# Huber loss of two 8192 x 8192 arrays: row tiles in bf16 over three engines, replaced by flat tiles in f32 on one transfer queue

## The chip, the cores and the metric

The kernel runs on one core of a Trainium2 chip. The metric is the device time of one execution in microseconds. A core has the engines DVE (vector), ACT (scalar functions), POOL (general purpose) and PE (matrix, not used here), and SP, which only issues transfers. Each engine works through its own list of instructions in order. Transfers between HBM and the on-chip memory (128 partitions) run on 16 transfer engines, fed from the queues of SP, ACT and POOL.

## The reference

```python
def reference(pred, target):
    delta = 1.0
    diff = pred - target
    abs_diff = np.abs(diff)
    return np.where(abs_diff <= delta, 0.5 * diff**2, delta * (abs_diff - 0.5 * delta))
```

Both inputs and the output are 8192 x 8192 f32, 268.44 MB each. So 536.87 MB are read and 268.44 MB written, and there are three or four elementwise steps per element. Both kernels compute 0.5 * min(|d|, 1)^2 + max(|d| - 1, 0), with d = pred - target.

## The kernel before

The arrays are taken in 64 row tiles of 128 rows x 8192 columns. A row tile is loaded in two halves of 4096 columns for each input (`emit_loads`, L46; 2.1 MB each, in f32). The first input and the first half of the second are issued by SP (L54, L56), the second half of the second by ACT. Each input has a pool of three such half buffers. POOL subtracts the halves into one bf16 tile `dfull` (L103), so everything behind it is in half precision. `dfull` has two buffers, the result tile `sfull` three.

For a row tile ACT takes the absolute value of `dfull` in place (L108) and DVE writes min(|d|, 1) to `sfull` (L109). One round later, in `do_tail` (L65), ACT squares `sfull` with the factor sqrt(0.5) (L68), ACT writes max(|d| - 1, 0) to `dfull` (L69) and DVE adds the two (L70). The store of `sfull` goes out from POOL's queue (L63), which casts it from bf16 to f32 on the way, a round later still.

Thus ACT's list in a round is L68 and L69 of one tile, then L108 of the next. L68 of that next tile waits for DVE's L109. POOL's subtraction needs a free `dfull`, that is, the end of L70 two tiles earlier; and SP's next loads need half buffers that POOL has read.

The last two row tiles (L117 to L226) are written out by hand in pieces of 2048 or 1024 columns, spread over ACT and DVE, so that the last stores are small.

Of the kernel before, what the change touches and what calls it, by code (L numbers as in the profile page):

```python
# [6 lines left out]


@with_exitstack
def kernel(  # L10
# [6 lines left out]
    nc = tc.nc  # L17
    P = 128
    fp32 = mybir.dt.float32
    bf16 = mybir.dt.bfloat16  # L20
    Alu = mybir.AluOpType
    Act = mybir.ActivationFunctionType

    n_rows, n_cols = pred.shape
    COLS = 4096
    n_ct = n_cols // COLS
    SQRT_HALF = 0.70710678118654752

    pred_t = pred.rearrange("(n p) m -> n p m", p=P)
    targ_t = target.rearrange("(n p) m -> n p m", p=P)  # L30
    out_t = out.rearrange("(n p) m -> n p m", p=P)
    n_rt = pred_t.shape[0]

    neg1 = nc.alloc_sbuf_tensor("huber_neg1_bf16", [P, 1], bf16)
    nc.gpsimd.memset(neg1.ap(), -1.0)

    pool_a = ctx.enter_context(tc.tile_pool(name="sbuf_a", bufs=3))
    pool_b = ctx.enter_context(tc.tile_pool(name="sbuf_b", bufs=3))
    pool_d = ctx.enter_context(tc.tile_pool(name="sbuf_d", bufs=2))
    pool_s = ctx.enter_context(tc.tile_pool(name="sbuf_s", bufs=3))  # L40

    loads = {}
    pending_tail = []
    pending_store = []

    def emit_loads(i):  # L46
        if i >= n_rt:
            return
        tl = []
        for j in range(n_ct):  # L50
            c0 = j * COLS
            a = pool_a.tile([P, COLS], fp32)
            b = pool_b.tile([P, COLS], fp32)
            nc.sync.dma_start(out=a, in_=pred_t[i, :, c0 : c0 + COLS])  # L54
            beng = nc.sync if j == 0 else nc.scalar
            beng.dma_start(out=b, in_=targ_t[i, :, c0 : c0 + COLS])  # L56
            tl.append((a, b))
        loads[i] = tl

    def flush(limit):  # L60
        while len(pending_store) > limit:
            r, pi = pending_store.pop(0)
            nc.gpsimd.dma_start(out=out_t[pi, :, :], in_=r)  # L63

    def do_tail(limit):  # L65
        while len(pending_tail) > limit:
            s, d, pi = pending_tail.pop(0)
            nc.scalar.activation(out=s, in_=s, func=Act.Square, scale=SQRT_HALF)  # L68
            nc.scalar.activation(out=d, in_=d, func=Act.Relu, bias=neg1.ap())  # L69
            nc.vector.tensor_tensor(out=s, in0=s, in1=d, op=Alu.add)  # L70
            pending_store.append((s, pi))

    def act_path(d, s):
        nc.scalar.activation(out=d, in_=d, func=Act.Abs)
        nc.vector.tensor_scalar(
            out=s, in0=d, scalar1=1.0, scalar2=None, op0=Alu.min
        )
        nc.scalar.activation(out=s, in_=s, func=Act.Square, scale=SQRT_HALF)
        nc.scalar.activation(out=d, in_=d, func=Act.Relu, bias=neg1.ap())
        nc.vector.tensor_tensor(out=s, in0=s, in1=d, op=Alu.add)  # L80

    def dve_path(d, s):
        nc.vector.tensor_scalar(
            out=s, in0=d, scalar1=-1.0, scalar2=1.0, op0=Alu.max, op1=Alu.min
        )
        nc.vector.scalar_tensor_tensor(
            out=d, in0=s, scalar=-0.5, in1=d, op0=Alu.mult, op1=Alu.add
        )
        nc.vector.tensor_tensor(out=s, in0=s, in1=d, op=Alu.mult)

    emit_loads(0)
    for i in range(n_rt - 2):
        dfull = pool_d.tile([P, n_cols], bf16)
        sfull = pool_s.tile([P, n_cols], bf16)

        emit_loads(i + 1)

        do_tail(0)

        for j in range(n_ct):  # L100
            c0 = j * COLS
            a, b = loads[i][j]
            nc.gpsimd.tensor_tensor(  # L103
                out=dfull[:, c0 : c0 + COLS], in0=a, in1=b, op=Alu.subtract
            )
        del loads[i]

        nc.scalar.activation(out=dfull, in_=dfull, func=Act.Abs)  # L108
        nc.vector.tensor_scalar(  # L109
            out=sfull, in0=dfull, scalar1=1.0, scalar2=None, op0=Alu.min,  # L110
        )

        flush(1)

        pending_tail.append((sfull, dfull, i))

    i62 = n_rt - 2  # L117
    i63 = n_rt - 1
    H = n_cols // 2

    d62 = pool_d.tile([P, n_cols], bf16, tag="dfull")
    s62 = pool_s.tile([P, n_cols], bf16, tag="sfull")

    emit_loads(i63)
    do_tail(0)

    for j in range(n_ct):
        c0 = j * COLS
        a, b = loads[i62][j]
        nc.gpsimd.tensor_tensor(  # L130
            out=d62[:, c0 : c0 + COLS], in0=a, in1=b, op=Alu.subtract
        )
    del loads[i62]

    flush(1)

    Q = 2048
    dq = [d62[:, k * Q : (k + 1) * Q] for k in range(4)]
    sq = [s62[:, k * Q : (k + 1) * Q] for k in range(4)]
    nc.scalar.activation(out=dq[0], in_=dq[0], func=Act.Abs)  # L140
    nc.vector.tensor_scalar(out=sq[0], in0=dq[0], scalar1=1.0, scalar2=None, op0=Alu.min)  # L141
    nc.vector.tensor_scalar(  # L142
        out=sq[1], in0=dq[1], scalar1=-1.0, scalar2=1.0, op0=Alu.max, op1=Alu.min
    )
    nc.scalar.activation(out=sq[0], in_=sq[0], func=Act.Square, scale=SQRT_HALF)  # L145
    nc.scalar.activation(out=dq[0], in_=dq[0], func=Act.Relu, bias=neg1.ap())
    nc.vector.scalar_tensor_tensor(  # L147
        out=dq[1], in0=sq[1], scalar=-0.5, in1=dq[1], op0=Alu.mult, op1=Alu.add
    )
    nc.vector.tensor_tensor(out=sq[0], in0=sq[0], in1=dq[0], op=Alu.add)  # L150
    nc.scalar.activation(out=dq[2], in_=dq[2], func=Act.Abs)
    nc.vector.tensor_tensor(out=sq[1], in0=sq[1], in1=dq[1], op=Alu.mult)  # L152
    nc.vector.tensor_scalar(out=sq[2], in0=dq[2], scalar1=1.0, scalar2=None, op0=Alu.min)  # L153
    nc.vector.tensor_scalar(
        out=sq[3], in0=dq[3], scalar1=-1.0, scalar2=1.0, op0=Alu.max, op1=Alu.min
    )
    nc.scalar.activation(out=sq[2], in_=sq[2], func=Act.Square, scale=SQRT_HALF)  # L157
    nc.scalar.activation(out=dq[2], in_=dq[2], func=Act.Relu, bias=neg1.ap())  # L158
    nc.vector.scalar_tensor_tensor(  # L159
        out=dq[3], in0=sq[3], scalar=-0.5, in1=dq[3], op0=Alu.mult, op1=Alu.add  # L160
    )
    nc.vector.tensor_tensor(out=sq[2], in0=sq[2], in1=dq[2], op=Alu.add)  # L162
    nc.vector.tensor_tensor(out=sq[3], in0=sq[3], in1=dq[3], op=Alu.mult)

    d63 = pool_d.tile([P, n_cols], bf16, tag="dfull")
    s63 = pool_s.tile([P, n_cols], bf16, tag="sfull")

    bounds = [0, 2048, 4096, 6144, 7168, 8192]
    chunks = [(bounds[k], bounds[k + 1]) for k in range(len(bounds) - 1)]

    flush(0)
    for k, (lo, hi) in enumerate(chunks):
        a, b = loads[i63][lo // COLS]
        o0, o1 = lo % COLS, (hi - 1) % COLS + 1
        nc.gpsimd.tensor_tensor(  # L175
            out=d63[:, lo:hi], in0=a[:, o0:o1], in1=b[:, o0:o1], op=Alu.subtract
        )
        if 1 <= k <= 4:
            nc.gpsimd.dma_start(  # L179
                out=out_t[i62, :, (k - 1) * Q : k * Q], in_=sq[k - 1]  # L180
            )
    del loads[i63]

    d0, s0 = d63[:, 0:2048], s63[:, 0:2048]
    d1, s1 = d63[:, 2048:4096], s63[:, 2048:4096]
    d2, s2 = d63[:, 4096:6144], s63[:, 4096:6144]
    d3, s3 = d63[:, 6144:7168], s63[:, 6144:7168]
    d4, s4 = d63[:, 7168:8192], s63[:, 7168:8192]

    def st(lo, hi, s):  # L190
        nc.gpsimd.dma_start(out=out_t[i63, :, lo:hi], in_=s)  # L191

    nc.scalar.activation(out=d0, in_=d0, func=Act.Abs)
    nc.vector.tensor_scalar(out=s0, in0=d0, scalar1=1.0, scalar2=None, op0=Alu.min)  # L194
    nc.scalar.activation(out=s0, in_=s0, func=Act.Square, scale=SQRT_HALF)  # L195
    nc.scalar.activation(out=d0, in_=d0, func=Act.Relu, bias=neg1.ap())
    nc.vector.tensor_scalar(
        out=s1, in0=d1, scalar1=-1.0, scalar2=1.0, op0=Alu.max, op1=Alu.min
    )
    nc.vector.scalar_tensor_tensor(  # L200
        out=d1, in0=s1, scalar=-0.5, in1=d1, op0=Alu.mult, op1=Alu.add
    )
    nc.vector.tensor_tensor(out=s1, in0=s1, in1=d1, op=Alu.mult)
    st(2048, 4096, s1)
    nc.vector.tensor_tensor(out=s0, in0=s0, in1=d0, op=Alu.add)
    st(0, 2048, s0)
    nc.scalar.activation(out=d2, in_=d2, func=Act.Abs)
# [49 lines left out]
```

## Time and profile before

| | us |
|---|---|
| median of 4 runs | 1923.01 (1922.92 to 1923.35) |
| profiled execution | 1923.17 |
| its span, first to last instruction | 1921.4 |
| DVE / ACT / POOL busy | 850.0 / 1326.3 / 1289.0 |

The profile belongs to the one profiled execution, which took 1.8 us more than its span. In its rows, a group is a line of the kernel, an engine and an operation, with output and input by the names in the program. "SPq" and "ACTq" are the sequencers that issue transfers. The share of the transfer engines is the mean over 16 of them of the time that their packets took; packets overlap, so it can be over 1. GB/s is what they moved. A window is a stretch of the span in microseconds.

### The profile page before, as it was taken

Reading aid. Unit: us, or ns where it says so; the run is one execution under the profiler, and the core shown is the slowest. Engines: PE = TensorE matmul, PEld = TensorE weight load, DVE = VectorE, ACT = ScalarE, POOL = GpSimd, SP = SyncE. Lnnn points to the kernel's source line nnn. Section 1 sums busy time; section 2 is a strip of 40 time slices with the busy share of each in tenths; the row PEclk is TensorE's granted clock in tenths of the full one; section 3 lists DMA queues with packets and bytes.
Section 4 is the critical chain, followed back from the end, with each engine's and each line's share of the span. In section 5 each row is a group of like instructions: output and inputs, shape, how many; then the busy total and the mean of one; then the engine's idle time right before and its main releaser. Section 6 shows DMA issues by size and latency. Waiting matters only on the chain.

```text
span 1921.4 us, 1430 instructions
## 1 busy us (share of the span) xinstructions
DVE 850.0 (44%) x146; ACT 1326.3 (69%) x202; POOL 1289.0 (67%) x207
## 2 busy tenths in 40 slices
DVE  0344354453443534534435345344353443444566
ACT  2866767668677676686776866767768667676674
POOL 5686676766866767667677676676766866767664
DMA  9999999999999999999999999999999999999996
GB/s 405 378 416 427 426 427 422 424 424 427 425 424 426 424 426 422 424 426 426 424 422 427 425 425 423 424 424 425 425 423 425 426 423 425 425 422 424 426 429 272
DMA packets 47099, 805.42 MB, mean 419 GB/s; under 512 B 5232, under 2 KB 5232, under 8 KB 5488
## 3 DMA queue, kind: packets, MB, share of 16 engines
q1 hardware_dynamic: 27648, 402.67, 53.9%
q0 software_dynamic: 10224, 268.44, 32.9%
q10 hardware_dynamic: 9216, 134.22, 16.3%
q14 instruction: 11, 0.09, 0.0%
HBM read 536.87 MB, written 268.44 MB: 419 GB/s over the span
## 4 chain that ended last, share of the span: by engine, by line
ACT 50%; DVE 29%; issue 17%; DMA 2%; POOL 1%; ACTq 0%; POOLq 0%; SPq 0%; DVEq 0%
DVE sfull L109 27%; ACT dfull L108 22%; ACT sfull L68 22%; ACT dfull L69 5%; DMA out_dram<-sfull 1%; DMA b<-in_target_dram 1%; POOL dfull L103 1%; DVE s L153 1%; DVE s L142 0%; DVE sfull L70 0%; DVE s L194 0%; DVE d L147 0%; DVE d L159 0%; ACT d L158 0%; ACT s L195 0%
## 5 line engine op out<-in xcount | busy, mean ns | idle before, releaser
L103 POOL TENSOR_TENSOR dfull<-a,b 128x4096 bf16<-128x4096 f32 x124 | 1213.8, 9803 | 588.0 <-issue 558.9
L68 ACT ACTIVATE sfull<-sfull 128x8192 bf16<-128x8192 bf16 x62 | 435.9, 7030 | 532.9 <-DVE sfull L109 532.9
L70 DVE TENSOR_TENSOR sfull<-sfull,dfull 128x8192 bf16<-128x8192 bf16 x62 | 274.4, 4426 | 860.6 <-ACT dfull L69 860.6
L109 DVE TENSOR_SCALAR sfull<-dfull 128x8192 bf16<-128x8192 bf16 x62 | 528.7, 8528 | 194.8 <-ACT dfull L108 194.8
L108 ACT ACTIVATE dfull<-dfull 128x8192 bf16<-128x8192 bf16 x62 | 434.8, 7013 | 33.1 <-POOL dfull L103 33.1
L69 ACT ACTIVATE dfull<-dfull,huber_neg_bf 128x8192 bf16<-128x8192 bf16 x62 | 440.6, 7106 | 0.0
L63 POOL DMA_DIRECT2D out_dram<-sfull x62 | 35.7, 575 | 3.8 <-DVE sfull L70 3.8
L130 POOL TENSOR_TENSOR d<-a,b 128x4096 bf16<-128x4096 f32 x2 | 19.6, 9839 | 9.5 <-issue 9.5
L175 POOL TENSOR_TENSOR d<-a,b 128x2048 bf16<-128x2048 f32 (+1 forms) x5 | 18.1, 3643 | 0.1
L191 POOL DMA_DIRECT2D out_dram<-s x5 | 2.7, 540 | 11.7 <-DVE s L217 5.9
L153 DVE TENSOR_SCALAR s<-d 128x2048 bf16<-128x2048 bf16 x1 | 9.8, 9845 | 0.0
L179 POOL DMA_DIRECT2D out_dram<-s x4 | 2.2, 551 | 10.6 <-DVE s L152 4.2
L142 DVE TENSOR_SCALAR s<-d 128x2048 bf16<-128x2048 bf16 x1 | 8.2, 8181 | 1.1 <-DMA out_dram<-sfull 1.1
L195 ACT ACTIVATE s<-s 128x2048 bf16<-128x2048 bf16 x1 | 1.9, 1910 | 8.1 <-DVE s L194 8.1
L162 DVE TENSOR_TENSOR s<-s,d 128x2048 bf16<-128x2048 bf16 x1 | 6.1, 6054 | 2.7 <-ACT d L158 2.7
L157 ACT ACTIVATE s<-s 128x2048 bf16<-128x2048 bf16 x1 | 1.9, 1910 | 6.0 <-DVE s L153 6.0
L145 ACT ACTIVATE s<-s 128x2048 bf16<-128x2048 bf16 x1 | 1.9, 1910 | 4.1 <-DVE s L141 4.1
L194 DVE TENSOR_SCALAR s<-d 128x2048 bf16<-128x2048 bf16 x1 | 3.3, 3276 | 0.0
L147 DVE SCALAR_TENSOR_TENSOR d<-s,d 128x2048 bf16<-128x2048 bf16 x1 | 2.3, 2292 | 0.0
L159 DVE SCALAR_TENSOR_TENSOR d<-s,d 128x2048 bf16<-128x2048 bf16 x1 | 2.3, 2286 | 0.0
L200 DVE SCALAR_TENSOR_TENSOR d<-s,d 128x2048 bf16<-128x2048 bf16 x1 | 2.3, 2277 | 0.0
L108 ACT ACT_TABLE_LOAD x1 | 1.3, 1283 | 1.2 <-PEq L241 1.2
(32 smaller groups left out, 34.7 us busy)
## 6 DMA issues: line engine op xcount, KB each, us to landing
a<-in_pred_dram SPq DMA_DIRECT2D x128, 2048.0 KB, 18.0
out_dram<-sfull POOLq DMA_DIRECT2D x62, 4096.0 KB, 20.1
b<-in_target_dram ACTq DMA_DIRECT2D x64, 2048.0 KB, 13.8
b<-in_target_dram SPq DMA_DIRECT2D x64, 2048.0 KB, 24.6
out_dram<-s POOLq DMA_DIRECT2D x7, 1024.0 KB, 4.9
out_dram<-s POOLq DMA_DIRECT2D x2, 512.0 KB, 4.9
```

The costliest lines, as they stand in the source:

```text
L63: nc.gpsimd.dma_start(out=out_t[pi, :, :], in_=r)
L68: nc.scalar.activation(out=s, in_=s, func=Act.Square, scale=SQRT_HALF)
L69: nc.scalar.activation(out=d, in_=d, func=Act.Relu, bias=neg1.ap())
L70: nc.vector.tensor_tensor(out=s, in0=s, in1=d, op=Alu.add)
L103: nc.gpsimd.tensor_tensor(out=dfull[:, c0 : c0 + COLS], in0=a, in1=b, op=Alu.subtract)
L108: nc.scalar.activation(out=dfull, in_=dfull, func=Act.Abs)
L109: nc.vector.tensor_scalar(out=sfull, in0=dfull, scalar1=1.0, scalar2=None, op0=Alu.min,)
L130: nc.gpsimd.tensor_tensor(out=d62[:, c0 : c0 + COLS], in0=a, in1=b, op=Alu.subtract)
L142: nc.vector.tensor_scalar(out=sq[1], in0=dq[1], scalar1=-1.0, scalar2=1.0, op0=Alu.max, op1=Alu.min)
L153: nc.vector.tensor_scalar(out=sq[2], in0=dq[2], scalar1=1.0, scalar2=None, op0=Alu.min)
L162: nc.vector.tensor_tensor(out=sq[2], in0=sq[2], in1=dq[2], op=Alu.add)
L175: nc.gpsimd.tensor_tensor(out=d63[:, lo:hi], in0=a[:, o0:o1], in1=b[:, o0:o1], op=Alu.subtract)
```

## The change

The function is rewritten. Each array is taken as one flat row of 67,108,864 elements and cut into 43 tiles: 42 of 128 partitions x 12288 columns (6.29 MB) and a last one of 128 x 8192. A partition of a tile is one unbroken stretch of HBM. There are two buffers for each input, of 48 KB per partition, and no others but a constant; everything stays f32, and the result is written over the first input's tile.

All transfers, the stores too, are issued by SP, in f32 without a cast. For a tile, `load` brings the second input whole and the first in two halves of 6144 columns; for the first tile and the last four, both come in halves, turn by turn. The store is one transfer for a whole tile, and for the last tile one for each piece of 2048 columns.

A tile is computed in pieces of 2048 columns. `first` has DVE subtract (L73) and clamp to -1..1 (L74), and ACT take Abs (L77), Relu of that minus 1 (L78) and Square of the clamped value (L79), all in place. `second` has DVE do 0.5 * b + a (L84). The order on SP, DVE and ACT is as written: `second` of a piece comes after `first` of the piece two further on. After a tile's last `second` SP gets its store and then the loads of the tile two further on. POOL only sets constants at the start.

The core of the diff:

```diff
-    pool_a = ctx.enter_context(tc.tile_pool(name="sbuf_a", bufs=3))
-    pool_b = ctx.enter_context(tc.tile_pool(name="sbuf_b", bufs=3))
-    pool_d = ctx.enter_context(tc.tile_pool(name="sbuf_d", bufs=2))
-    pool_s = ctx.enter_context(tc.tile_pool(name="sbuf_s", bufs=3))
+    flat = [x.rearrange("r c -> (r c)") for x in (pred, target, out)]
+    tiles = []
+    at = 0
+    while at < total:
+        w = min(ROW, (total - at) // P)
+        tiles.append((at, w))
+        at += P * w
+    pool_a = ctx.enter_context(tc.tile_pool(name="pool_a", bufs=DEPTH))
+    pool_b = ctx.enter_context(tc.tile_pool(name="pool_b", bufs=DEPTH))
...
-            nc.sync.dma_start(out=a, in_=pred_t[i, :, c0 : c0 + COLS])
-            beng = nc.sync if j == 0 else nc.scalar
-            beng.dma_start(out=b, in_=targ_t[i, :, c0 : c0 + COLS])
+        for at, to in cuts(w, w // 2 if i < 1 or i > n - 5 else w):
+            nc.sync.dma_start(out=B[i][:, at:to], in_=dram(1, i)[:, at:to])
+            for lo, hi in cuts(to - at, min(w // 2, to - at)):
+                lo, hi = at + lo, at + hi
+                nc.sync.dma_start(out=A[i][:, lo:hi], in_=dram(0, i)[:, lo:hi])
...
-            nc.gpsimd.dma_start(out=out_t[pi, :, :], in_=r)
+    def store(i, lo, hi):
+        nc.sync.dma_start(out=dram(2, i)[:, lo:hi], in_=A[i][:, lo:hi])
...
-            nc.gpsimd.tensor_tensor(
-                out=dfull[:, c0 : c0 + COLS], in0=a, in1=b, op=Alu.subtract
-            )
-        nc.scalar.activation(out=dfull, in_=dfull, func=Act.Abs)
-        nc.vector.tensor_scalar(
-            out=sfull, in0=dfull, scalar1=1.0, scalar2=None, op0=Alu.min,
-        )
+    def first(i, lo, hi):
+        a, b = A[i][:, lo:hi], B[i][:, lo:hi]
+        nc.vector.tensor_tensor(out=a, in0=a, in1=b, op=Alu.subtract)
+        nc.vector.tensor_scalar(
+            out=b, in0=a, scalar1=-1.0, scalar2=1.0, op0=Alu.max, op1=Alu.min
+        )
+        nc.scalar.activation(out=a, in_=a, func=Act.Abs)
+        nc.scalar.activation(out=a, in_=a, func=Act.Relu, bias=neg1)
+        nc.scalar.activation(out=b, in_=b, func=Act.Square)
-            nc.scalar.activation(out=s, in_=s, func=Act.Square, scale=SQRT_HALF)
-            nc.scalar.activation(out=d, in_=d, func=Act.Relu, bias=neg1.ap())
-            nc.vector.tensor_tensor(out=s, in0=s, in1=d, op=Alu.add)
+    def second(i, lo, hi):
+        a, b = A[i][:, lo:hi], B[i][:, lo:hi]
+        nc.vector.scalar_tensor_tensor(
+            out=a, in0=b, scalar=0.5, in1=a, op0=Alu.mult, op1=Alu.add
+        )
...
+    with tc.manual_schedule(engines={Eng.SP, Eng.DVE, Eng.Activation}):
+        for i in range(DEPTH):
+            load(i)
+        for i in range(n):
+            w = tiles[i][1]
+            late = []
+            for lo, hi in cuts(w, PIECE):
+                first(i, lo, hi)
+                late.append((lo, hi))
+                if len(late) > 2:
+                    second(i, *late[0])
+                    if i == n - 1:
+                        store(i, *late[0])
+                    late.pop(0)
+            for lo, hi in late:
+                second(i, lo, hi)
+                if i == n - 1:
+                    store(i, lo, hi)
+            if i < n - 1:
+                store(i, 0, w)
+                if i + DEPTH < n:
+                    load(i + DEPTH)
```

with `P = 128`, `ROW = 12288`, `PIECE = 2048`, `DEPTH = 2`.

How the lists stand, at two places. First SP's list at the start of the kernel before; the numbers behind a name tell buffers apart, `a` is the first input, `b` the second, and the stores are not here but in POOL's list.

```order
L54 DMA a_68<-in_pred_dram 128x4096
L56 DMA b_69<-in_target_dram 128x4096
L54 DMA a_72<-in_pred_dram 128x4096
L54 DMA a_78<-in_pred_dram 128x4096
L56 DMA b_79<-in_target_dram 128x4096
L54 DMA a_82<-in_pred_dram 128x4096
L54 DMA a_92<-in_pred_dram 128x4096
```

SP's list of the changed kernel, from the second tile's loads on; `a_68` and `b_69` are the first tile.

```order
L62 DMA b_75<-in_target_dram 128x12288
L65 DMA a_74<-in_pred_dram 128x6144 x2
L68 DMA out_0_dram<-a_68 128x12288
L62 DMA b_117<-in_target_dram 128x12288
L65 DMA a_116<-in_pred_dram 128x6144 x2
L68 DMA out_0_dram<-a_74 128x12288
L62 DMA b_159<-in_target_dram 128x12288
```

The stores moved from POOL's list into SP's, each ahead of the loads of the tile that takes over its buffer, and the load halves of ACT's list are in it too.

Next DVE's list at the start of the kernel before, where a row tile has two instructions:

```order
L109 TENSOR_SCALAR sfull_77<-dfull_76 128x8192
L70 TENSOR_TENSOR sfull_77<-sfull_77,dfull_76 128x8192
L109 TENSOR_SCALAR sfull_91<-dfull_90 128x8192
L70 TENSOR_TENSOR sfull_91<-sfull_91,dfull_90 128x8192
L109 TENSOR_SCALAR sfull_108<-dfull_107 128x8192
```

And DVE's list of the changed kernel, from the end of the first tile (`a_68`) into the second (`a_74`):

```order
L73 TENSOR_TENSOR a_68<-a_68,b_69 128x2048
L74 TENSOR_SCALAR b_69<-a_68 128x2048
L84 SCALAR_TENSOR_TENSOR a_68<-b_69,a_68 128x2048 x3
L73 TENSOR_TENSOR a_74<-a_74,b_75 128x2048
L74 TENSOR_SCALAR b_75<-a_74 128x2048
```

The subtraction moved here from POOL, and a tile ends with three multiply-adds in a row ahead of the next tile's first subtraction.

More of the change, by code (lines that the diff above doesn't have):

```diff
@@ L4 @@
 import concourse.tile as tile
-from concourse import bass_utils, mybir
+from concourse import mybir
 from concourse._compat import with_exitstack
+P = 128
+ROW = 12288
+PIECE = 2048
+DEPTH = 2
 @with_exitstack
@@ L17 @@
     nc = tc.nc
-    P = 128
-    fp32 = mybir.dt.float32
-    bf16 = mybir.dt.bfloat16
+    f32 = mybir.dt.float32
     Alu = mybir.AluOpType
     Act = mybir.ActivationFunctionType
[L24 to L34, printed above, removed]
@@ L35 @@
-    nc.gpsimd.memset(neg1.ap(), -1.0)
-    pool_a = ctx.enter_context(tc.tile_pool(name="sbuf_a", bufs=3))
-    pool_b = ctx.enter_context(tc.tile_pool(name="sbuf_b", bufs=3))
-    pool_d = ctx.enter_context(tc.tile_pool(name="sbuf_d", bufs=2))
-    pool_s = ctx.enter_context(tc.tile_pool(name="sbuf_s", bufs=3))
[L42 to L53, printed above, removed]
-            nc.sync.dma_start(out=a, in_=pred_t[i, :, c0 : c0 + COLS])
-            beng = nc.sync if j == 0 else nc.scalar
-            beng.dma_start(out=b, in_=targ_t[i, :, c0 : c0 + COLS])
-            tl.append((a, b))
-        loads[i] = tl
@@ L60, in flush @@
-    def flush(limit):
-        while len(pending_store) > limit:
-            r, pi = pending_store.pop(0)
-            nc.gpsimd.dma_start(out=out_t[pi, :, :], in_=r)
[L65 to L71, printed above, removed]
@@ L73, in act_path, with dram @@
-    def act_path(d, s):
-        nc.scalar.activation(out=d, in_=d, func=Act.Abs)
+    Eng = mybir.EngineType
+    total = pred.shape[0] * pred.shape[1]
+    flat = [x.rearrange("r c -> (r c)") for x in (pred, target, out)]
[5 more added lines that the diff above has]
+        at += P * w
+    n = len(tiles)
+    def dram(x, i):
+        at, w = tiles[i]
+        return flat[x][at : at + P * w].rearrange("(p m) -> p m", p=P)
@@ new lines, with cuts, load @@
+    const = ctx.enter_context(tc.tile_pool(name="const", bufs=1))
+    pool_a = ctx.enter_context(tc.tile_pool(name="pool_a", bufs=DEPTH))
+    pool_b = ctx.enter_context(tc.tile_pool(name="pool_b", bufs=DEPTH))
+    neg1 = const.tile([P, 1], f32)
+    nc.vector.memset(neg1, -1.0)
+    A, B = {}, {}
+    def cuts(w, step):
+        return [(lo, min(lo + step, w)) for lo in range(0, w, step)]
+    def load(i):
+        A[i] = pool_a.tile([P, ROW], f32, name="a")
+        B[i] = pool_b.tile([P, ROW], f32, name="b")
+        w = tiles[i][1]
[4 more added lines that the diff above has]
+                nc.sync.dma_start(out=A[i][:, lo:hi], in_=dram(0, i)[:, lo:hi])
@@ L75, in act_path @@
+    def store(i, lo, hi):
[3 more added lines that the diff above has]
+        nc.vector.tensor_tensor(out=a, in0=a, in1=b, op=Alu.subtract)
         nc.vector.tensor_scalar(
-            out=s, in0=d, scalar1=1.0, scalar2=None, op0=Alu.min
+            out=b, in0=a, scalar1=-1.0, scalar2=1.0, op0=Alu.max, op1=Alu.min
         )
-        nc.scalar.activation(out=s, in_=s, func=Act.Square, scale=SQRT_HALF)
@@ L79, in act_path @@
-        nc.scalar.activation(out=d, in_=d, func=Act.Relu, bias=neg1.ap())
-        nc.vector.tensor_tensor(out=s, in0=s, in1=d, op=Alu.add)
-    def dve_path(d, s):
-        nc.vector.tensor_scalar(
-            out=s, in0=d, scalar1=-1.0, scalar2=1.0, op0=Alu.max, op1=Alu.min
-        )
-        nc.vector.scalar_tensor_tensor(
-            out=d, in0=s, scalar=-0.5, in1=d, op0=Alu.mult, op1=Alu.add
-        )
-        nc.vector.tensor_tensor(out=s, in0=s, in1=d, op=Alu.mult)
-    emit_loads(0)
@@ L92 @@
[L92 to L103, printed above, removed]
-                out=dfull[:, c0 : c0 + COLS], in0=a, in1=b, op=Alu.subtract
-            )
-        del loads[i]
-        nc.scalar.activation(out=dfull, in_=dfull, func=Act.Abs)
-        nc.vector.tensor_scalar(
-            out=sfull, in0=dfull, scalar1=1.0, scalar2=None, op0=Alu.min,
-        )
-        flush(1)
-        pending_tail.append((sfull, dfull, i))
@@ L117 @@
[L117 to L207, printed above, removed]
@@ L208 @@
-    nc.vector.tensor_scalar(out=s2, in0=d2, scalar1=1.0, scalar2=None, op0=Alu.min)
-    nc.scalar.activation(out=s2, in_=s2, func=Act.Square, scale=SQRT_HALF)
-    nc.scalar.activation(out=d2, in_=d2, func=Act.Relu, bias=neg1.ap())
-    nc.vector.tensor_scalar(
-        out=s4, in0=d4, scalar1=-1.0, scalar2=1.0, op0=Alu.max, op1=Alu.min
-    )
-    nc.vector.scalar_tensor_tensor(
-        out=d4, in0=s4, scalar=-0.5, in1=d4, op0=Alu.mult, op1=Alu.add
-    )
-    nc.vector.tensor_tensor(out=s2, in0=s2, in1=d2, op=Alu.add)
@@ L218 @@
-    st(4096, 6144, s2)
-    nc.scalar.activation(out=d3, in_=d3, func=Act.Abs)
-    nc.vector.tensor_scalar(out=s3, in0=d3, scalar1=1.0, scalar2=None, op0=Alu.min)
-    nc.scalar.activation(out=s3, in_=s3, func=Act.Square, scale=SQRT_HALF)
-    nc.scalar.activation(out=d3, in_=d3, func=Act.Relu, bias=neg1.ap())
-    nc.vector.tensor_tensor(out=s4, in0=s4, in1=d4, op=Alu.mult)
-    st(7168, 8192, s4)
-    nc.vector.tensor_tensor(out=s3, in0=s3, in1=d3, op=Alu.add)
-    st(6144, 7168, s3)
+        nc.scalar.activation(out=a, in_=a, func=Act.Abs)
@@ new lines, in first @@
+        nc.scalar.activation(out=a, in_=a, func=Act.Relu, bias=neg1)
[4 more added lines that the diff above has]
+            out=a, in0=b, scalar=0.5, in1=a, op0=Alu.mult, op1=Alu.add
+        )
+    with tc.manual_schedule(engines={Eng.SP, Eng.DVE, Eng.Activation}):
+        for i in range(DEPTH):
+            load(i)
+        for i in range(n):
+            w = tiles[i][1]
+            late = []
[15 more added lines that the diff above has]
+                    load(i + DEPTH)
```

## The prediction

> **What bounds the kernel now.** I read the page first.
>
> ```profile
> span 1921.4 us, 1430 instructions
> DVE 850.0 (44%) x146; ACT 1326.3 (69%) x202; POOL 1289.0 (67%) x207
> DMA  9999999999999999999999999999999999999996
> GB/s 405 378 416 427 426 427 422 424 424 427 425 424 426 424 426 422 424 426 426 424 422 427 425 425 423 424 424 425 425 423 425 426 423 425 425 422 424 426 429 272
> HBM read 536.87 MB, written 268.44 MB: 419 GB/s over the span
> ```
>
> No engine is busy over 70%, the transfer engines are busy in every slice, and 805.31 MB cross. That reads as a kernel bound by transfers, with a weak second slice and a weak last one. The chain of waits over two steady tiles says something else, so I read it with the timeline of the same stretch.
>
> ```profile
> 1008.69 7.02 ACT dfull L108
> 1015.72 0.02 issue
> 1015.74 8.62 DVE sfull L109
> 1024.35 0.02 issue
> 1024.38 7.03 ACT sfull L68
> 1031.41 1.70 ACT dfull L69
> 1033.11 5.22 issue
> 1038.33 7.02 ACT dfull L108
> ```
>
> ```profile
> 1031.31 7.11 ACT L69 ACTIVATE dfull<-dfull,huber_neg_bf 128x8192 bf16<-128x8192 bf16 x1
> 1008.82 4.43 DVE L70 TENSOR_TENSOR sfull<-sfull,dfull 128x8192 bf16<-128x8192 bf16 x1 [14.11 <-ACT dfull L69]
> 1013.39 19.64 POOL L103 TENSOR_TENSOR dfull<-a,b 128x4096 bf16<-128x4096 f32 x2 [9.47 <-issue]
> ```
>
> The "issue" of 5.22 us is only the rest of L69, which runs from 1031.31 to 1038.42. So ScalarE goes round a closed ring: Abs of this tile (L108), wait for the vector minimum (L109), Square (L68) and Relu (L69), Abs of the next tile. One turn is 1038.33 - 1008.69 = 29.64 us and moves one row tile of 12.58 MB: 424.5 GB/s. POOL starts its subtractions 0.14 us after L70 ends, for it needs the half-precision buffer that L70 frees, and the loads wait for POOL. The steady rate is therefore set by this ring, not by the transfer engines alone; they are so nearly full that the page can't tell. What they can do is read from windows.
>
> ```profile
> core 0: us, DVE busy (x) ACT busy (x) POOL busy (x), PEclk, DMA share, GB/s
> 0.00:5.00 5.00, 0.00 (x0) 1.28 (x1) 0.30 (x5) 1.00 0.68 246
> 5.00:35.00 30.00, 0.00 (x0) 0.00 (x0) 17.05 (x2) 1.00 1.00 429
> 16.00:26.00 10.00, 0.00 (x0) 0.00 (x0) 8.05 (x1) 1.00 1.01 431
> 50.00:55.00 5.00, 0.00 (x0) 5.00 (x2) 5.00 (x1) 1.00 1.02 436
> 1000.00:1296.30 296.30, 130.30 (x20) 209.59 (x31) 201.54 (x31) 1.00 1.04 425
> 1862.00:1866.00 4.00, 3.96 (x3) 4.00 (x1) 1.46 (x2) 1.00 1.00 422
> 1880.00:1921.40 41.40, 26.55 (x15) 17.83 (x11) 17.99 (x12) 1.00 0.63 246
> 1914.00:1918.00 4.00, 0.00 (x0) 0.00 (x0) 0.00 (x0) 1.00 0.96 328
> ```
>
> Loads with nothing in their way run at 429 to 431, against 425 in ten steady tiles. At 425 all bytes would take 805.31 / 0.425 = 1894.8 us, so the ring's rate is most of the time and 26.6 us are lost at the ends: the last 41.4 us, at 246, lose 41.4 x (1 - 246/425) = 17.4 of them, the first 5 us 2.1, and the start-up of the rings most of the rest. The profiled execution took 1923.17 us, 1.8 more than its span; the median is 1923.01, so it stands for the runs.
>
> **The change, part by part.** The bytes to and from HBM stay 805.31 MB. POOL's subtraction, its stores and the old ring are gone. In their place stand 42 wide tiles (three times 6.29 MB each) and a last one of 8192 columns, with two buffers per input. Two things can set the pace: the transfers, or the pass of DVE and ACT over a tile.
>
> *The pass.* Per 2048 columns DVE does a subtraction, a clamp and a multiply-add, ACT does Abs, Relu and Square, all in f32. The trace has the same shape in bf16.
>
> ```profile
> L147 DVE SCALAR_TENSOR_TENSOR d<-s,d 128x2048 bf16<-128x2048 bf16 x1 | 2.3, 2292 | 0.0
> L163 DVE TENSOR_TENSOR s<-s,d 128x2048 bf16<-128x2048 bf16 x1 | 1.2, 1225 | 0.0
> L154 DVE TENSOR_SCALAR s<-d 128x2048 bf16<-128x2048 bf16 x1 | 0.7, 689 | 0.0
> L140 ACT ACTIVATE d<-d 128x2048 bf16<-128x2048 bf16 x1 | 1.9, 1892 | 0.0
> L146 ACT ACTIVATE d<-d,huber_neg_bf 128x2048 bf16<-128x2048 bf16 x1 | 2.0, 1986 | 0.0
> L145 ACT ACTIVATE s<-s 128x2048 bf16<-128x2048 bf16 x1 | 1.9, 1910 | 4.1 <-DVE s L141 4.1
> ```
>
> ACT: 1.89 + 1.99 + 1.91 = 5.79 us per piece; I carry it over to f32, since the three functions cost nearly the same; the pass could grow by 3 us, 0.5 per piece, before it passes the 43.8 of the transfers below. DVE in f32 has no row. Subtraction lies between 1.23 and 2.29; I take 2.29, the slower row, because f32 is twice the bytes of L163. The clamp lies between 0.69 and 2.29; I take 1.23, about twice L154. Multiply-add 2.29. DVE then has 5.81 us per piece, level with ACT. Each ACT piece waits for its own clamp, and the last multiply-add waits for the last Square, so the pass is 3.52 + 6 x 5.79 + 2.29 = 40.6 us. With the clamp at 0.69 it is 40.1; at 2.29 DVE leads (6.87 x 6 and one wait) and it is about 42.5.
>
> The Trainium skill, in "VectorE: DVE Perf Modes", section on the perf-mode tier table, has 1227 ns for an f32 tensor_scalar and 2293 for an f32 tensor_tensor at this size. No run here shows them yet; by them the pass is the same 40.6.
>
> *The transfers.* At 431 GB/s a wide tile takes 18.87 MB / 0.431 = 43.8 us, longer than the pass. They stay fed if each order arrives before the queue runs dry. The last A half of a tile lands 7.3 us after its first, at time D. The pass starts at D - 7.3, ends at D + 33.4, and its store is then issued; the queue still holds work until D + 43.8, so 10 us are spare. SP waits for that store to land before it issues the A loads behind it (same buffer), but the B load of 14.6 us is already queued and covers this. On SP a store queued ahead of a load therefore blocks nothing that could run; ACT issues no transfers any more, and POOL none.
>
> *The rate.* This is the one term that matters, and no row has f32 rows of 24 or 48 KB, in one queue. Below is 425, what the mixed traffic ran at; above is 436, the best window here. I take 431, the loads' own rate in 16 KB rows. The stores' queue gives no reason to go lower:
>
> ```profile
> q0 software_dynamic: 10224, 268.44, 32.9%
> q10 hardware_dynamic: 9216, 134.22, 16.3%
> ```
>
> 32.9% of 16 engines over 1921.4 us is 10114 us for 268.44 MB, or 26.5 GB/s per engine and 425 for sixteen, beside other queues and with small end pieces in it; q10's loads give 5011 us for 134.22 MB, 429. The Trainium skill, "DMA: Bandwidth & Descriptors", section on where 436 GB/s comes from, puts the ceiling at 435.2. By it the floor of the time is an estimated 1850.4 + 10.2 = 1860.6 us; the 436 window agrees with it to one part in 500.
>
> *The ends.* Front: 5 x (1 - 246/429) = 2.1 us, as now, for the first loads go out as early. The second slice's loss goes: the two tiles loaded at the start hold 25.2 MB, 58 us of work, and the first pass, in halves, is done by about 58. Tail: call D the landing of the last load. The loads of tile 41 ended 34.1 us earlier (one store, 8.39 MB of loads), its first half 14.6 before that, so its pass ends at D - 48.7 + 40.6 = D - 8.1. The last pass, of four pieces, takes 3.52 + 4 x 5.79 + 2.29 = 29.0 and ends at D + 20.9. By then the store of tile 41 (14.6) and three of four last pieces (2.43 each) are nearly gone; the last one lands 4.9 us after its issue, by these rows:
>
> ```profile
> out_dram<-s POOLq DMA_DIRECT2D x7, 1024.0 KB, 4.9
> 1912.57 0.53 POOL L191 DMA_DIRECT2D out_dram<-s  x1 [0.40 <-DVE s L225]
> ```
>
> So D + 25.8, where transfers without a gap would end at D + 24.3: 1.5 us. Behind the last landing, 1912.57 + 4.9 = 1917.5, the span of before runs on for 3.9 us; I keep that, and 1.8 outside the span. Sum of the ends: 2.1 + 1.5 + 3.9 + 1.8 = 9.3, and 0.9 for some ten wakes between engines of 0.02 to 0.14 us in these last passes: 10.2.
>
> **Sum:** 805.31 / 0.431 = 1868.5, and 10.2, makes 1879 us (2.3% off). At 425 it is 1905, at 429 1887, at 436 1857. A clamp of 2.29 hides in the middle and costs about 8 us at the end, where the last four passes run back to back.
>
> **The rivals.**
>
> *The rate stays 425* because reads and writes that share the engines reach no more, and ring and ceiling only happened to agree. For it: the share is 1.04 in every steady window. Against it: 429 to 431 when no ring is in the way. Time: 1905, still faster, as the ends alone lose 16 us less. Chance 0.18.
>
> *Stores alone are slow (slower).* Now a store runs in its stretch of the one queue, with no load beside it. The only such place here is the window 1914 to 1918, at 328 with a share of 0.96. At 328 the stores take 268.44 / 0.328 = 818 us and the loads 536.87 / 0.431 = 1246, in all 2074. It decides from where stores fall under about 401: 268.44 / 0.401 + 1246 + 10 = 1925. Against it: those last pieces are 0.5 and 1 MB in 4 to 8 KB rows, and the queue is draining; large stores gave 425 above. With it goes a single ring that can't fill the engines: below 421 overall (805.31 / (1923.2 - 10.2)) the gain is gone. Chance 0.08. The Trainium skill, same page, section on the iDMA fabric, reports 408.7 for one load stream issued from SP with 4 KiB rows. By that it would take 805.31 / 0.4087 + 10.2 = 1981 us, an estimate; no run here has such short rows, and the 16 KB rows above ran faster.
>
> *The pass becomes the bound (slower).* L109 takes 8.53 us for 8192 columns:
>
> ```profile
> L109 DVE TENSOR_SCALAR sfull<-dfull 128x8192 bf16<-128x8192 bf16 x62 | 528.7, 8528 | 194.8 <-ACT dfull L108 194.8
> ```
>
> Four times L154 would be 2.76, so it is stretched 3.1 times. If the transfers do that, the clamp becomes 3.8 us, DVE has 8.4 per piece, and 256 pieces take 2150 us, some 2175 in all. It decides at a pass of 44.5 us: 17 + 42 x 44.5 + 29 + 11 = 1926. Against it: L154 ran in 0.69 inside the window 1862 to 1866, with transfers at 422 and POOL mostly idle, while L109 overlaps POOL's subtraction. So POOL stretches it, and POOL has no work after the change. Chance 0.04.
>
> **How the numbers follow.** The forecast, bound by transfers at 429 to 436, has 0.68; its own range is 1857 to 1888. The other three cases have 0.30, and 0.02 is left for a rate of 420 to 422 that ends level. From both ends of the rate and of the clamp (1905 + 8) the range is 1860 to 1912. About 0.2% is what a measurement here can tell from no change. Faster: 0.68 + 0.18 + 0.01 = 0.87; same 0.03; slower 0.10.
>
> **What would show it.** Right: the slices of GB/s even from the second on at 429 or more, DVE and ACT each idle some 3 us per tile for a load, SP's waits for DVE covered, the clamp near 1.2 us. Wrong in the rate: even slices at 425 or less. Wrong in the pass: gaps in the transfer share while DVE or ACT is busy without a break. Wrong on stores: GB/s that falls every 44 us, for 15.

## The result, and the profile after

The changed kernel takes 1878.06 us (median of 8 runs, 1876.58 to 1879.23), the kernel before 1923.12 us (12 runs, 1922.92 to 1923.37). The ratio is 0.9765, 95% interval 0.9756 to 0.9775: 2.35% faster, 45 us. The forecast was 1879. The profiled execution took 1878.28 us, 2.1 more than its span.

The page of the changed kernel, in the same order as before:

```profile
span 1876.2 us, 1983 instructions
DVE 1452.5 (77%) x769; ACT 1440.1 (77%) x769; POOL 0.2 (0%) x4
DMA  9999999999999999999999999999999999999998
GB/s 412 432 429 433 432 435 436 431 431 434 432 435 431 432 431 432 431 434 433 434 435 430 436 432 432 434 434 427 433 432 433 437 432 435 432 431 413 423 414 369
HBM read 536.87 MB, written 268.44 MB: 429 GB/s over the span
```

The dip of the second slice (378) is gone and the middle stands at 427 to 437. But the last four slices, not one, are weak: 413, 423, 414, 369. That was not forecast. The windows put numbers on it:

```profile
0.00:5.00 5.00, 0.06 (x1) 0.00 (x0) 0.20 (x4) 1.00 0.69 226
5.00:1690.00 1685.00, 1309.40 (x693) 1294.90 (x692) 0.00 (x0) 1.00 1.00 433
1690.00:1825.00 135.00, 108.65 (x59) 110.72 (x60) 0.00 (x0) 1.00 1.00 417
1825.00:1876.00 51.00, 34.40 (x18) 34.51 (x19) 0.00 (x0) 1.00 0.90 372
```

The groups by line give the prices of the f32 instructions that no row of before showed (busy, mean ns of one, then idle time ahead of them and who ended it):

```profile
L73 DVE TENSOR_TENSOR a<-a,b 128x2048 f32<-128x2048 f32 x256 | 585.1, 2285 | 177.9 <-DMA a<-in_pred_dram 177.8
L74 DVE TENSOR_SCALAR b<-a 128x2048 f32<-128x2048 f32 x256 | 314.1, 1227 | 8.9
L84 DVE SCALAR_TENSOR_TENSOR a<-b,a 128x2048 f32<-128x2048 f32 x256 | 585.1, 2287 | 228.2 <-ACT b L79 228.2
L77 ACT ACTIVATE a<-a 128x2048 f32<-128x2048 f32 x256 | 485.5, 1896 | 399.2 <-DVE b L74 399.2
L78 ACT ACTIVATE a<-a,neg 128x2048 f32<-128x2048 f32 x256 | 512.5, 2002 | 8.4
L79 ACT ACTIVATE b<-b 128x2048 f32<-128x2048 f32 x256 | 484.5, 1893 | 0.0
```

One tile in the timeline, from store to store:

```profile
1013.34 0.34 SPq L68 DMA_DIRECT2D out_dram<-a  x1
1013.78 0.38 SPq L62 DMA_DIRECT2D b<-in_target_dram  x1
1017.14 2.29 DVE L73 TENSOR_TENSOR a<-a,b 128x2048 f32<-128x2048 f32 x1 [3.83 <-DMA a<-in_pred_dram]
1039.82 0.80 SPq L65 DMA_DIRECT2D a<-in_pred_dram  x2
1054.67 2.29 DVE L84 SCALAR_TENSOR_TENSOR a<-b,a 128x2048 f32<-128x2048 f32 x1 [3.34 <-ACT b L79]
1056.99 0.34 SPq L68 DMA_DIRECT2D out_dram<-a  x1
```

A pass runs from 1017.14 to 1056.96, 39.8 us. DVE waits 3.83 us for the load ahead of it, so the transfers set the pace: 1056.99 - 1013.34 = 43.65 us a tile, 18.87 MB in that time, 432 GB/s. SP waits 26 us for the store to land before it issues the first input's loads, and the queue still holds work all that time: the share from 5 to 1690 us is 1.00.

### The profile page after: what moved, and what is told of

Read it like the earlier page. It is cut to its first block, busy times and chain, and to the rows that moved or that the text cites. A ratio compares the mean times of both kernels' runs of the same rounds, so it can differ in the third digit from the quotient of the medians.

```text
span 1876.2 us, 1983 instructions
## 1 busy us (share of the span) xinstructions
DVE 1452.5 (77%) x769; ACT 1440.1 (77%) x769; POOL 0.2 (0%) x4
## 4 chain that ended last, share of the span: by engine, by line
DMA 54%; ACT 36%; DVE 7%; issue 2%; ACTq 0%; SPq 0%; DVEq 0%
DMA out_dram<-a 29%; DMA a<-in_pred_dram 25%; ACT a L77 12%; ACT b L79 12%; ACT a L78 11%; DVE a L73 3%; DVE a L84 3%; DVE b L74 1%; ACTq L135 0%; SPq L62 0%; DVEq L73 0%; SPq L65 0%
## 5 line engine op out<-in xcount | busy, mean ns | idle before, releaser
L77 ACT ACTIVATE a<-a 128x2048 f32<-128x2048 f32 x256 | 485.5, 1896 | 399.2 <-DVE b L74 399.2
L84 DVE SCALAR_TENSOR_TENSOR a<-b,a 128x2048 f32<-128x2048 f32 x256 | 585.1, 2287 | 228.2 <-ACT b L79 228.2
L73 DVE TENSOR_TENSOR a<-a,b 128x2048 f32<-128x2048 f32 x256 | 585.1, 2285 | 177.9 <-DMA a<-in_pred_dram 177.8
L78 ACT ACTIVATE a<-a,neg 128x2048 f32<-128x2048 f32 x256 | 512.5, 2002 | 8.4
L79 ACT ACTIVATE b<-b 128x2048 f32<-128x2048 f32 x256 | 484.5, 1893 | 0.0
L74 DVE TENSOR_SCALAR b<-a 128x2048 f32<-128x2048 f32 x256 | 314.1, 1227 | 8.9
```

What stands on the lines that cost most here:

```text
L73: nc.vector.tensor_tensor(out=a, in0=a, in1=b, op=Alu.subtract)
L74: nc.vector.tensor_scalar(out=b, in0=a, scalar1=-1.0, scalar2=1.0, op0=Alu.max, op1=Alu.min)
L77: nc.scalar.activation(out=a, in_=a, func=Act.Abs)
L78: nc.scalar.activation(out=a, in_=a, func=Act.Relu, bias=neg1)
L79: nc.scalar.activation(out=b, in_=b, func=Act.Square)
L84: nc.vector.scalar_tensor_tensor(out=a, in0=b, scalar=0.5, in1=a, op0=Alu.mult, op1=Alu.add)
```

## The experiments

All are compared with the kernel before on the same chip; times are medians. The theory was that the ring of ACT and DVE held the old kernel back, that the longer rows give the rest, and that the order of the one queue hides the waits. The main rival was that the kind of queue (one hardware queue, no casting stores) makes the gain.

**The old ring without two of its members** (`e1_short_ring`).

```diff
-            nc.scalar.activation(out=d, in_=d, func=Act.Relu, bias=neg1.ap())
-            nc.vector.tensor_tensor(out=s, in0=s, in1=d, op=Alu.add)
             pending_store.append((s, pi))
```

> The kernel before with the Relu (L69) and the add (L70) left out of its first 62 tiles, so its output lacks the linear part there; every transfer stays. Theory: the ring of ACT and DVE set the pace at 29.63 us a tile, and without two of its members the transfers do: 16 KB rows at 429 GB/s, 29.3 us a tile, 62 x 0.3 = 19 us less, about 1904. Rival (transfers were the limit before, through their queues and the casting stores): the tile stays at 29.6 us and 425 GB/s, 1918 to 1923.

Measured: 1889.48 us (1889.14 to 1889.66), ratio 0.9825 (0.9808 to 0.9841). Page, windows and waits:

```profile
GB/s 403 424 432 426 432 435 426 433 429 432 434 427 431 430 430 432 430 436 427 428 433 429 430 433 428 434 428 431 431 430 434 432 427 432 430 433 429 430 432 306
205.00:1005.00 800.00, 61.93 (x27) 383.39 (x55) 497.81 (x83) 1.00 1.06 431
POOL dfull L101 <- DMA b<-in_target_dram: 374.4, 36, 19.9
```

With the same three queues, the same casting stores and the same rows, the rate rises from 425 to 431, and POOL now waits for loads. That is 33.7 us, of the 45 that the change gains and more than the 19 expected: the tile takes 12.58 / 0.431 = 29.2 us and not 29.3, and the weak second slice goes too (378 to 424). The rival falls.

**Shorter rows** (`e2_rows16k`).

```diff
-            nc.sync.dma_start(out=B[i][:, at:to], in_=dram(1, i)[:, at:to])
-            for lo, hi in cuts(to - at, min(w // 2, to - at)):
-                lo, hi = at + lo, at + hi
-                nc.sync.dma_start(out=A[i][:, lo:hi], in_=dram(0, i)[:, lo:hi])
+            for x, t in ((1, B[i]), (0, A[i])):
+                for lo, hi in cuts(to - at, 4096):
+                    lo, hi = at + lo, at + hi
+                    nc.sync.dma_start(out=t[:, lo:hi], in_=dram(x, i)[:, lo:hi])
```

> The changed kernel with each load cut into transfers of 4096 columns (16 KB rows, as before the change), stores unchanged, the second input still ahead of the first. Theory (the rate follows the row length): loads at 429 instead of 433, 536.87 / 0.429 - 536.87 / 0.433 = 11.6 us more, about 1889, at 431 to 432 in the middle. Rival (one hardware queue without casts is what helps): no change, 1876 to 1880. If short rows are what pulls the last four tiles down to 412, the middle falls to some 415 and the time to 1945.

Measured: 1886.28 us (1885.83 to 1886.78), ratio 0.9808 (0.9794 to 0.9823).

```profile
205.00:1005.00 800.00, 621.22 (x330) 615.41 (x330) 0.00 (x0) 1.00 1.00 430
```

8.2 us more than the changed kernel, 430 for 433, somewhat less than the 11.6 expected. The edit raises the number of transfers too, but the records of the single packets point to the rows: one of 16 KB takes 611 ns (median) and one of 48 KB 1815, which is 429 and 433 GB/s for 16 engines. Short rows in themselves don't pull the rate down to the 412 that the changed kernel has from 1690 to 1735 us.

**Stores on a queue of their own, and everything on POOL's** (`e4_stores_pool`, `e11_all_pool`). The first changes `nc.sync` to `nc.gpsimd` in `store` alone, the second in `load` and `store`; POOL's list then keeps the written order too.

> The changed kernel with its stores issued from POOL's queue, f32 without a cast as before. Theory (bytes and row lengths set the rate, not the queue): 431 to 434 GB/s in the middle and 1872 to 1885 us. Rival (the gain is that all traffic stands in one hardware queue): the rate falls to 425 and the time rises to 1900 or more.

> The changed kernel with every transfer issued from POOL's queue instead of SP's, in the same order. Theory (it is the one order that matters, not whose queue it is, and stores on a queue of their own lost 158 us by breaking it): 431 to 434 GB/s and 1875 to 1890 us. Rival (a queue fed by POOL is slower): under 428, above 1895.

Measured: 2034.91 us (2014.28 to 2037.22 in three runs, 2045.76 in a fourth that the ratio leaves out), ratio 1.0549 (1.0491 to 1.0608), for the first, slower than the kernel before; 1881.62 us (1881.15 to 1882.31), ratio 0.9784 (0.9768 to 0.9800), for the second. First run, timeline and windows of one tile:

```profile
1050.78 0.80 SPq L65 DMA_DIRECT2D a<-in_pred_dram  x2
1052.52 0.53 POOL L68 DMA_DIRECT2D out_dram<-a  x1 [39.20 <-DVE a L84]
1070.99 2.29 DVE L73 TENSOR_TENSOR a<-a,b 128x2048 f32<-128x2048 f32 x1 [18.76 <-DMA a<-in_pred_dram]
```

```profile
1044.00:1052.00 8.00, 4.36 (x2) 5.87 (x4) 0.00 (x0) 1.00 0.39 135
1060.00:1080.00 20.00, 8.94 (x5) 5.39 (x3) 0.00 (x0) 1.00 1.00 430
```

Second run, page and window:

```profile
q0 software_dynamic: 25920, 805.32, 99.7%
205.00:1005.00 800.00, 625.89 (x331) 620.51 (x333) 38.87 (x74) 1.00 1.00 433
```

In one order a queue fed by POOL carries 433, as SP's does. Both expectations of the first run missed: the rate itself holds (430 from 1060 to 1080), but a store that shares the engines with the next load lands when that load ends, the first input's loads wait for that landing at 1050.78 with nothing left behind them, and the transfers fall to 135 GB/s for 8 us. That stores stand in the queue ahead of the load that covers them is not a detail here: without it the new kernel is 112 us slower than the kernel before.

**Stores alone** (`e8_stores_only`): the 43 stores of two buffers that DVE fills once; no loads, no arithmetic.

> Only the 43 stores of the changed kernel, from two buffers set to zero; loads and arithmetic left out. Theory: stores alone run as fast as loads, 433 GB/s, 268.44 / 0.433 = 620 us and about 30 around them, most of it the two fills of the buffers. Rival of the prediction (stores alone are slow): under 401 GB/s, 670 us and more.

Measured in one run: 638.79 us; the window from 100 to 600 us:

```profile
100.00:600.00 500.00, 0.00 (x0) 0.00 (x0) 1.00 1.00 433
```

Stores alone run as fast as the mixed traffic of the changed kernel. The forecast's rival on stores is refuted.

**How much the pass can grow** (`e6_extra_clamp`), and **who stretched the clamp** (`e7_sub_pool`).

```diff
+        nc.vector.tensor_scalar(
+            out=b, in0=b, scalar1=-1.0, scalar2=1.0, op0=Alu.max, op1=Alu.min
+        )
         nc.scalar.activation(out=a, in_=a, func=Act.Abs)
```

```diff
-        nc.vector.tensor_tensor(out=a, in0=a, in1=b, op=Alu.subtract)
+        nc.gpsimd.tensor_tensor(out=a, in0=a, in1=b, op=Alu.subtract)
```

> The changed kernel with the clamp done twice, which changes no value: DVE gets 256 more instructions of 1.23 us, 314 us in all, 7.4 us a tile, of which about 3 show in the pass (40.6 to some 43.5). Theory (the pass is hidden under 43.6 us of transfers): nothing in the middle, up to 10 us at the end, where the last passes run back to back: 1880 to 1890. Rival (the pass, not the transfers, sets the pace): 43 x 3 = 129 us more, above 2000.

> The changed kernel with the subtraction back on POOL (f32). Theory (POOL's subtraction, not the transfers, stretched the clamp of the kernel before 3.1 times): the clamp rises from 1.23 to 3 us or more in the mean and the passes pass 43.6 us, so 1900 to 2050. Rival (transfers stretch it, or bf16 did): the clamp stays at 1.2 to 1.3.

Measured: 1880.96 us (1880.16 to 1882.51), ratio 0.9781 (0.9768 to 0.9795), with the second clamp, and 2129.15 us (two runs), ratio 1.1071 (1.1051 to 1.1091), with POOL's subtraction. Page of the first and groups of the second:

```profile
DVE 1762.4 (94%) x1025; ACT 1449.6 (77%) x769; POOL 0.2 (0%) x4
```

```profile
L73 POOL TENSOR_TENSOR a<-a,b 128x2048 f32<-128x2048 f32 x256 | 1452.6, 5705 | 639.0 <-DMA a<-in_pred_dram 634.6
L84 DVE SCALAR_TENSOR_TENSOR a<-b,a 128x2048 f32<-128x2048 f32 x256 | 994.1, 3890 | 192.2 <-ACT b L79 192.2
L74 DVE TENSOR_SCALAR b<-a 128x2048 f32<-128x2048 f32 x256 | 938.7, 3693 | 22.4 <-POOL a L73 22.4
```

310 us more of DVE work cost 2.9: the pass is hidden. With POOL at work beside DVE, the clamp takes 3.69 us for 1.23 and the multiply-add 3.89 for 2.29, at fewer bytes per second than before (379 GB/s over the span for 419). So POOL stretches them, not the transfers. POOL's own subtraction takes 5.7 us.

**The weak last slices.** They begin where loads come in halves. The first theory was that the first input's half then waits for a store with only 7.3 us of queue behind it, and that this costs 8 us.

`e3_whole_tail` drops the halves at the end (`w // 2 if i < 1 else w`); `e9_bbaa` keeps them but puts both halves of the second input first; `e5_piece_stores` stores the last six tiles piece by piece (`if i > n - 7: store(...)` behind each `second`); `e10_halves_all` has halves in every tile:

```diff
-        for at, to in cuts(w, w // 2 if i < 1 or i > n - 5 else w):
+        for at, to in cuts(w, w // 2):
```

> The changed kernel with the second input loaded whole in the last four tiles too. Theory (in the last four tiles the first half of the first input waits for a store to land with only half a transfer queued to cover it, so some transfer engines run dry): the stretch from 1690 to 1780 us goes from 412 to 423 back to 433, which wins some 8 us; but the last passes start up to 7 us later, so the time is 1873 to 1880. Rival (the dip belongs to the end itself, for instance to skew among the engines): the stretch stays near 415 and the time rises to some 1884.

> The changed kernel with the stores of its last six tiles issued piece by piece, each right behind its multiply-add, instead of one store per tile; loads in halves as they are. Theory (the dip is the wait of the first input for the landing of a whole store with too little queued behind it): most of a store has gone out by the time its tile ends, so the wait is short; the stretch from 1690 to 1825 us returns from 412 to 423 to about 430 and the time falls by 6 to 8 us to about 1871. Rival (the dip is the end's own skew): no change, 1876 to 1880.

> The changed kernel with the halves of its last four tiles in another order: both halves of the second input ahead of the first input's. Piece by piece stores could not tell, since behind the last piece again only half a transfer stood in the queue. Theory (what covers the wait for the store is what stands behind it in the queue): 14.6 us of it again, the stretch 1690 to 1825 at 430 or more, with the same 24 KB rows and the same count of transfers; the time as with whole loads, 1876 to 1881, since the passes start later. Rival (transfers in halves are what costs): the stretch stays at 412 to 420, and the time rises to some 1885.

> The changed kernel with the loads of all tiles in halves turn by turn, as in its last four. Theory: the dip of the last four tiles comes in every tile, 413 to 420 GB/s throughout, 38 x 1.5 to 2 us more, 1935 to 1955, and the gain of the change is gone. Rival (the dip belongs to the end): 1875 to 1882.

Measured: 1879.87 (1879.36 to 1880.10), ratio 0.9775 (0.9760 to 0.9789); 1878.98 (1878.42 to 1879.39), 0.9770 (0.9757 to 0.9783); 1880.12 (1879.51 to 1881.05), 0.9776 (0.9762 to 0.9791); 1879.97 (1877.50 to 1882.17), 0.9775 (0.9760 to 0.9789). Windows of whole loads, then of the other order of halves:

```profile
1690.00:1825.00 135.00, 106.27 (x57) 105.27 (x57) 0.00 (x0) 1.00 1.00 432
1825.00:1876.00 51.00, 37.21 (x20) 40.26 (x22) 0.00 (x0) 1.00 0.76 325
```

```profile
1690.00:1825.00 135.00, 106.15 (x56) 105.15 (x57) 0.00 (x0) 1.00 1.00 431
1825.00:1876.00 51.00, 36.71 (x20) 39.75 (x22) 0.00 (x0) 1.00 0.79 334
```

and of halves in every tile:

```profile
205.00:1005.00 800.00, 623.66 (x329) 618.18 (x331) 0.00 (x0) 1.00 1.00 431
1690.00:1825.00 135.00, 105.76 (x57) 104.90 (x57) 0.00 (x0) 1.00 1.00 432
1825.00:1876.00 51.00, 35.01 (x18) 35.81 (x20) 0.00 (x0) 1.00 0.91 376
```

With more behind the wait the stretch recovers, in the same 24 KB rows, as the theory said. Stores in pieces changed nothing (413 GB/s from 1690 to 1825 us): the theory had expected a gain, though again only half a transfer stands behind the last piece. And halves in every tile don't dip at all in that stretch, against the theory's 1935 to 1955. So the theory in that form is wrong.

The theory has engines run dry, and the dip doesn't look like that. Where the queue ran dry above, the share fell to 0.39; here it stays at 1.00. Three short stretches of the changed kernel hold over half of the loss. Their windows stand below one undisturbed stretch:

```profile
1735.00:1755.00 20.00, 13.00 (x7) 16.18 (x9) 0.00 (x0) 1.00 1.00 429
1715.00:1722.00 7.00, 6.93 (x5) 4.60 (x3) 0.00 (x0) 1.00 1.00 355
1762.00:1768.00 6.00, 5.73 (x4) 5.97 (x4) 0.00 (x0) 1.00 1.02 385
1806.00:1812.00 6.00, 5.96 (x4) 5.97 (x4) 0.00 (x0) 1.00 1.09 377
```

The records of the packets themselves, which no view lists, show rows of 24 KB that take 1.0 to 2.4 us there for the usual 0.91, in a transfer that had stood in the queue for 20 us. From 1690 to 1825 us 109 of 1518 such rows are over 1.0 us; in the same stretch none of 768 are with whole loads, 1 of 1519 with the other order and 6 of 1536 with halves in every tile. Why rows lengthen there is open.

The records show one difference from the run with halves in every tile. A transfer ends with 16 small writes, one per engine. In the changed kernel they lie 1.0 us apart for the first transfer, 3.0 at 440 us, 4.7 at 1050 and 6.6 at 1660: the engines drift apart. With halves in every tile the spread stays between 4.0 and 5.4 from 800 us on; with whole loads it goes on to 7.1. So the bursts go with halves that start at a wide spread, but no run shows that the spread makes them.

The last of the 16 writes, that of the last engine at the time, tells what the dip costs. Set against an even 433 GB/s, the last engine is 10.3 us behind at 1695.8 us and 15.2 behind when the last load lands at 1850.9: the stretch costs it 5 us. With whole loads that load lands at 1846.5, 4.4 us earlier, but the store of the last tile but one is then issued at 1845.2 instead of 1839.3, and the last landing comes 31 us after the last load and not 24. What the rate wins, the later passes lose, as the expectation of `e3_whole_tail` had it. Halves in every tile lose on the way instead: the last engine is 13.2 us behind at 1698.7 us, and the last load lands at 1850.9 there too. So no run without the dip is faster.

The drift itself was not tested, but its steps have a companion in the records: the packets of 8 KB on the instruction queue (`q14 instruction: 15, 0.12, 0.0%` on the page). Between 200 and 1690 us the spread of the changed kernel grows in four jumps of 0.7 to 1.0 us, in transfers that land at 719, 1025, 1331 and 1594 us, and a packet of that queue starts 3 to 4 us before each (715.8, 1021.1, 1327.3, 1589.9). No other step of the spread is over 0.2 us in that time; eight more such packets bring none. Stores alone stay within 0.4 us; they have no loads beside them, and no such packet after the start either, so that run can't tell the two apart.

**No gap between the last passes** (`e12_carry`): whole loads at the end, and `second` of a tile's last pieces behind `first` of the next tile's, from the fifth last tile on.

```diff
-            for lo, hi in late:
-                second(i, lo, hi)
...
+            if i < n - 5 or i == n - 1:
+                while late:
+                    finish()
```

(`finish` does the oldest piece's `second`, and behind a tile's last piece its store and the next loads.)

> The changed kernel with whole loads in the last four tiles, and with the last multiply-adds of a tile, from the fifth last tile on, behind the first pieces of the next tile, so that ACT does not run empty between the last passes (some 5.8 us each). Theory: the rate keeps 433 to the end and the passes no longer hold up the last stores, 4 to 9 us less than the changed kernel: 1869 to 1874. Rival (the end is bound by landings, not by passes): 1876 to 1880.

Measured: 1901.19 us (1900.50 to 1902.01), ratio 0.9886 (0.9871 to 0.9901), 23 us slower than the changed kernel. Timeline and window:

```profile
1716.79 2.29 DVE L73 TENSOR_TENSOR a<-a,b 128x2048 f32<-128x2048 f32 x1 [13.99 <-DMA a<-in_pred_dram]
1728.24 0.34 SPq L68 DMA_DIRECT2D out_dram<-a  x1
```

```profile
1720.00:1730.00 10.00, 9.96 (x6) 9.55 (x6) 0.00 (x0) 1.00 0.23 96
```

The store of a tile now waits for the next tile's first load and two of its pieces, 11.5 us after that load. The 10 us that the forecast found spare are overspent, and the queue runs dry once a tile. Both expectations missed the place: neither passes nor landings, but the store's time of issue.

## Why the prediction was right

- **The bound of before.** The ring set the pace, not the transfers: shown by `e1_short_ring`, at 33.7 us; going back to shorter rows costs 8.2 of the rest (`e2_rows16k`). The page alone (share 1.04, 425 GB/s) could not tell.
- **The pass.** 40.6 us forecast, 39.8 measured; subtraction 2.285, clamp 1.227, multiply-add 2.287, ACT 5.79. ACT's records overlap by some 0.1 us each, so that its six pieces take 33.9 us, 5.65 each; that is the difference. The Trainium skill's 1227 and 2293 ns ("VectorE: DVE Perf Modes", section on the perf-mode tier table) agree with the trace's 1227 and 2285.
- **The cover.** 10 us spare for the store's issue. In the trace a store is issued at 1013.34, and the next tile's last load lands at 1020.6 on the first engine and at 1025.3 on the last: 7.3 to 12.0 us. `e6_extra_clamp`, with a pass of 41.9 us, used some 2 to 3 of them, for 2.9 us more in the whole time; `e12_carry` overspent them.
- **The rate: mis-sized.** 431 forecast, 433 in the middle, and so 1859.8 us for the bytes and not 1868.5.
- **The ends: mis-sized the other way.** 10.2 forecast, 1878.28 - 1859.83 = 18.45 measured at that rate. The front is 2.4 for 2.1. The stretch up to the last load costs the last engine 5.0, for which the sum had nothing: the step "even slices from the second on" failed there. Behind the last load the sum had 1.5 + 3.9 + 0.9 = 6.3. The last landing came 24.3 us after it, where the 10.49 MB left take 24.2 at 433, and the span ended 1.0 later: 1.1 in all. Outside the span it was 2.1 for 1.8. The other 7.9 had built up before 1695.8 us: the last engine was 5.0 us behind the mean of the 16 by then, and the rest is the start and the rounding of 433.
- **The luck in it.** The two errors, 8.7 us less and 8.2 more, cancel. Counted by the last engine, the 704.64 MB between its landings at 62.2 and 1695.8 us went at 431.3, which leaves 1867 us for the bytes and 11 for the ends, nearly the forecast's two terms. But the forecast took its 431 from windows of loads and not from a lagging engine, and in its ends a tail that was 5 us too long stood for a dip of 5 us that it didn't foresee. The mechanism was right; that the time came within 1 us is luck.
- **The rivals.** A ceiling of 425: refuted, 430 to 433 in every kernel without the ring whose queue is kept fed. Slow stores or a single queue: refuted, 433 alone and together. The pass as the bound: refuted for this kernel, and shown to be what it becomes with POOL's subtraction beside DVE.

No version had a lower median than the changed kernel.

## What to carry to other kernels

A transfer share of 1.0 does not show that transfers set the pace: follow the chain of waits round one tile, and compare the steady rate with a stretch in which nothing but the queue limits it. Where one buffer serves load and store, what matters is what stands in the queue behind the store that is waited for, and when that store is issued; a second queue, or a later store, can cost more than every rate that is gained. The mean rate of 16 engines that drift apart flatters the middle of a kernel: the landing of the last engine tells what a dip costs, and a mended dip has to be set against what the mend costs elsewhere (here 4.4 us won and 6.7 lost).

## What the runs showed of the hardware

The price of a row: in the packet records of the changed kernel rows of 8, 16, 24 and 48 KB take 309, 611, 913 and 1815 ns (medians), about 301 for every 8 KB and 8 for the row. The 16 engines drift 6.6 to 7.1 us apart in 1700 us of mixed traffic (`after`, `e3_whole_tail`) and stay within 0.4 us of one another under stores alone. A multiply-add with two inputs on DVE is stretched by a subtraction on POOL too, 3.89 us for 2.29 (`e7_sub_pool`), as is the clamp, 3.69 for 1.23.
